# Normed rows and gated products of a two-layer encoder stored in the order in which TensorE loads them

## The chip, the core and the metric

The kernel runs on one core of a Trainium2 chip. The metric is the device time of one execution in microseconds (us); lower is better. The kernel before was run three times, with a median of 1843.3 us (1842.94 to 1844.39).

## What is computed

Two layers of an encoder over 512 frames of 1024 numbers, all in 32-bit floats. Each layer has an attention half (one input projection, retention, differential attention and gated linear attention, one output projection) and a second half, a mixture of 32 SwiGLU experts in 8 groups of 4. Only the second half is touched by the change. Cut to what matters:

```python
h2 = (rms_norm(x, norm2_g[l]) * (1.0 + sc2) + sh2).reshape(B_ * S_, D)
idx, gates = route(h2, router_w, router_b)      # best group, then its best 2 experts
...
def expert_block(args):
    toks, gts, e = args
    xb = h_pad[toks]
    u = jax.nn.silu(xb @ w_gate[e]) * (xb @ w_up[e])
    return (u @ w_down[e]) * gts[:, None]
...
x = x + gt2 * y
```

An expert has weights of 1024x512 (gate), 1024x512 (up) and 512x1024 (down).

## The kernel before, in words

The 512 frames lie in four tiles of 128 frames, frames on the partitions. In each layer the work around the change goes through these stages.

**Residual and routing.** For each tile i the output projection is finished, added to X, squared and summed, and `norm(i)` makes the reciprocal root r2. `route(i)` (from line 1127) then makes the router's scores on VectorE and ScalarE. In it the normed rows X*r2 are written as two parts of the type fp32r, whose products are summed: the high part `xh` (line 1139, ScalarE, one operation of 1024 columns a tile) and the low part `xl`. For tiles 0 and 1 VectorE makes `xl` (line 1141, 1024 columns); for tiles 2 and 3 ScalarE writes X*r2 once more into `xf` (line 1147, two halves of 512) and GpSimd subtracts `xh` (line 1148). From the chosen groups VectorE ranks the groups by size and makes the one-hot matrix `Pt` that puts each frame at a place of its group (line 1298).

**The gather.** `hs`, the normed inputs in the order of the places and turned, is made by matmuls (line 1358): for each of 2 halves of the places (384 columns each), each of 8 blocks k of features, each tile and each of xh and xl one 128x128 stationary operand from the normed rows, with 384 columns of `Pt` streamed past it. That is 128 matmuls in a layer. Eight of them fill one of three PSUM banks, which ScalarE (line 1364, even k) or VectorE (line 1362, odd k) empties. The stationary operand of block k takes every fourth column of a half row:

```python
T.matmul(b, xx[:, i].rearrange("p (q t k) -> p q k t", q=2, k=4)[:, k // 4, k % 4],
         Pt[:, i, c * HP:(c + 1) * HP], ...)
```

so that features which lie next to each other in the weights' rows come from one row of HBM (a partition then holds 4 whole rows of the weight matrix). Then the same `Pt` is streamed past the 4 gate columns of each tile (line 1602).

**The experts.** 32 experts run in a fixed order, alternately one of a large group (places 128 wide, "wide", weights split in two parts by ScalarE and VectorE, three matmuls a block) and one of a small group (64 places, "narrow", the two halves of the columns packed side by side). SyncE issues the weights (line 1435), 1 MB a transfer, into a ring of buffers `R`; `H` are the split parts. For expert e: the gate product, Silu on ScalarE (`es`), the up product, and in `up_part` the gated product `eu` = up * gate weight * Silu in one VectorE operation (line 1489, 512 columns for a wide, 256 for a narrow expert). `turn` transposes `eu` on TensorE halfway through the gate product of the next expert (4 transposes for a wide, 2 for a narrow one), again with a strided stationary operand (every second column), and the down product follows. When a group's four experts are done, `combine` puts its sums back on X: it runs in small steps between the next expert's matmuls, with matmuls against `ePT` and one VectorE addition for each (`u<-u,x`). After the first expert all four engines' instructions are kept in program order, recorded by one helper: they all carry line 122.

Of the kernel before, what the change touches and what calls it, by code (L numbers as in the profile page):

```python
# [15 lines left out]
AF = mybir.ActivationFunctionType  # L16
OP = mybir.AluOpType
# [5 lines left out]
DEPTH, S, D, NT, KD = 2, 512, 1024, 4, 8  # L23
# [116 lines left out]
def hybrid_trunk(ctx: ExitStack, tc: tile.TileContext, x, c, positions, w_mod, b_mod, norm1_g, norm2_g, w_in,  # L140
# [5 lines left out]
    V, A, G, T, SP = nc.vector, nc.scalar, nc.gpsimd, nc.tensor, nc.sync  # L146
# [26 lines left out]
    X = pool(xs, "x0").tile([128, NT, D])  # L173
# [9 lines left out]
    ident = cst("ident")  # L183
# [185 lines left out]
    for l in range(depth):  # L369
        first = l == 0  # L370
        with ExitStack() as ps:
# [104 lines left out]
            for k in range(KD):  # L476
                q, kk = divmod(k, 4)
# [643 lines left out]
            def norm(i):  # L1121
# [2 lines left out]
                V.tensor_scalar(ms, ms, 1.0 / D, EPS, op0=OP.mult, op1=OP.add)  # L1124
                rsqrt(r2s[:, i:i + 1], ms, 1)

            def route(i):

                r2 = r2s[:, i:i + 1]
                lt = rtile([128, NE], "lt")  # L1130
                if i < NT - 1:
                    V.tensor_copy(lt, lp[:, i, 0])
                    yield
                    V.tensor_add(lt, lt, lp[:, i, 1])
                    yield
                V.scalar_tensor_tensor(lt, lt if i < NT - 1 else lp[:, i, 0], r2, lsh, op0=OP.mult, op1=OP.add)
                sc = rtile([128, NE], "sc")
                act(sc, lt, AF.Exp, scale=-1.0)
                A.activation(xh[:, i], X[:, i], AF.Copy, scale=r2)
                if i < NT - 2:  # L1140
                    V.scalar_tensor_tensor(xl[:, i], X[:, i], r2, xh[:, i], op0=OP.mult, op1=OP.subtract)
                else:

                    for n in range(2):
                        cs_ = slice(n * 512, (n + 1) * 512)
                        xf = w2([128, 512], tag="sq", bufs=2)
                        A.activation(xf, X[:, i, cs_], AF.Copy, scale=r2)
                        G.tensor_sub(xl[:, i, cs_], xf, xh[:, i, cs_])
                yield
                V.tensor_scalar(sc, sc, 1.0, None, op0=OP.add)  # L1150
                yield
                V.reciprocal(sc, sc)
                yield
                bi = rtile([128, NG, 4], "bi")
                bif = bi.rearrange("p g e -> p (g e)")
                V.tensor_add(bif, sc, rb)
                yield

                u = rtile([128, NG, 6], "u")
                V.tensor_add(u[:, :, 0:3], bi[:, :, 0:3], bi[:, :, 1:4])  # L1160
                V.tensor_add(u[:, :, 3:5], bi[:, :, 0:2], bi[:, :, 2:4])
                V.tensor_add(u[:, :, 5:6], bi[:, :, 0:1], bi[:, :, 3:4])
                yield
                gs, r1 = rtile([128, NG], "gs"), rtile([128, 1], "r1")
                V.tensor_reduce(gs, u, axis=AX.X, op=OP.max)
                yield
                V.tensor_reduce(r1, gs, axis=AX.X, op=OP.max)
                yield
                V.scalar_tensor_tensor(gs, gs, r1, cst("gidx"), op0=OP.is_equal, op1=OP.mult)
                yield  # L1170
                V.tensor_reduce(r1, gs, axis=AX.X, op=OP.max)
                yield

                pen = rtile([128, NG], "pen")
                V.tensor_scalar(pen, cst("gidx"), r1, NEG, op0=OP.not_equal, op1=OP.mult)
                V.tensor_scalar(grp[:, i], cst("gidx"), r1, None, op0=OP.is_equal)

                T.matmul(pc[:, (i + 1) * NG:(1 + NT) * NG], cst("ones"),
                         grp[:, i, None, :].to_broadcast([128, NT - i, NG]), start=(i == 0), stop=False)
                chosen[i] = sc, bi, pen  # L1180
                yield
# [171 lines left out]
            for c in range(2):  # L1353
                for k in range(KD):
                    b = pbank("x", 3)[:, 0:HP]
                    for i in range(NT):
                        for n, xx in enumerate((xh, xl)):
                            T.matmul(b, xx[:, i].rearrange("p (q t k) -> p q k t", q=2, k=4)[:, k // 4, k % 4],
                                     Pt[:, i, c * HP:(c + 1) * HP], start=(i == 0 and n == 0), stop=(i == NT - 1 and n == 1))
                    dst = hs[:, k, c * HP:(c + 1) * HP]  # L1360
                    if k % 2:
                        V.tensor_scalar(dst, b, hcol[:, 0, k:k + 1], hcol[:, 1, k:k + 1], op0=OP.mult, op1=OP.add)
                    else:
                        A.activation(dst, b, AF.Identity, scale=hcol[:, 0, k:k + 1], bias=hcol[:, 1, k:k + 1])
# [96 lines left out]
            def wide(acc, src, e, amid=None):  # L1461

                r = where[e][0]
                for p in range(4):
                    hl = src.get()
                    for k in range(2):
                        start, stop = p == 0 and k == 0, p == 3 and k == 1
                        if r < NWIDE:
                            three(acc, xTs[r], 2 * p + k, hl, k * 512, start, stop)
                        else:  # L1470
                            halved(acc, hs[:, 2 * p + k, OFFS[r]:OFFS[r] + 64], hl, k * 512, 512, start, stop)
                    step()
                    if amid and p == 1:
                        amid()
# [6 lines left out]
            def up_part(src, e, gacc):  # L1481
                r, j = where[e]
                w = 512 if r < NWIDE else 256
                s = wm.tile([128, FE], tag="es")[:, 0:w]
                A.activation(s, gacc[:, 0:w], AF.Silu)
                acc = pbank("u")
                wide(acc, src, e)
                u_ = wm.tile([128, FE], tag="eu")[:, 0:w]
                V.scalar_tensor_tensor(u_, acc[:, 0:w], gcs[:, r, j:j + 1], s, op0=OP.mult, op1=OP.mult)
                return u_  # L1490

            def turn(u_, e):
                b = pbank("x", 3, [128, 4, 128])
                if where[e][0] < NWIDE:
                    for q in range(4):
                        T.transpose(b[:, q], u_.rearrange("p (q t k) -> p q k t", q=2, k=2)[:, q // 2, q % 2], ident)
                    uT = wm.tile([128, 2, 4, 128], F32R, tag="euT")
                    A.copy(uT[:, 0], b)
                    V.tensor_sub(uT[:, 1], b, uT[:, 0])
                else:  # L1500
                    for k in range(2):
                        T.transpose(b[:, k], u_.rearrange("p (t k) -> p k t", k=2)[:, k], ident)
                    uT = wm.tile([128, 2, 128], tag="euT64")
                    A.copy(uT, b[:, 0:2])
                return uT
# [274 lines left out]
```

## Time and profile before, and how to read them

| | |
|---|---|
| median of 3 runs | 1843.3 us |
| the profiled execution: its own time | 1843.05 us |
| its span, first to last instruction | 1841.2 us |
| busy: PE (matmuls), PEld (weight loads), DVE (VectorE), ACT (ScalarE) | 1765.0, 1270.0, 1095.8, 784.2 us |
| mean granted TensorE clock | 0.981 of 2.4 GHz |
| DMA | 512.12 MB, mean 278 GB/s |

Matmuls overlap in the trace and their ends are modelled, so a busy PE says little; the distance from one start to the next says what a matmul takes in a stream. With a group of n like instructions that lasts s in all, and d for one, that distance is (s - d)/(n - 1). A bracket behind a row is the idle time of the engine before it and what ended it. DVEq, SPq and so on are an engine's sequencer.

### The profile page before, as it was taken

To read this page: it belongs to the slowest core of one execution; us is meant where nothing else is said; L and a number is where in the kernel's file an instruction comes from. 1 tells how busy PE (TensorE), PEld (TensorE's weight loads), DVE (VectorE), ACT (ScalarE), POOL (GpSimd) and SP (SyncE) were. 2 spreads that over 40 slices of the span, in tenths; PEclk is the share of its full clock that TensorE was granted. 3 is DMA by queue.
4 is the path that set the end of the run, shared out by engine and by line. 5 is a ranking of instruction groups with operands and counts; after the bars stand their busy time and mean duration, and the time that the engine had idled before them with its cause. 6 is when DMAs were issued, how large, how long until landed. Compare 5 with 4: busy or idle time off the path is not lost. (4 is left out here: it accounts for less than half of the span.)

```text
span 1841.2 us, 28185 instructions
## 1 busy us (share of the span) xinstructions
PE 1765.0 (96%) x10891; PEld 1270.0 (69%) x10892; DVE 1095.8 (60%) x1968; ACT 784.2 (43%) x1207; POOL 89.4 (5%) x136
## 2 busy tenths in 40 slices
PE   5999999989999999999998999997999999999997
PEld 3866767768665666665748887986966666666673
DVE  3646664464547557566655778656455846756664
ACT  3344442343534443444523555443344444444350
POOL 1010000020000000000000110112000000000000
PEclk9999999998999999999998999998999999999998
DMA  9565547416999999999964211131789999999994
GB/s 333 166 213 191 171 160 226 164 73 253 359 423 378 392 423 367 415 422 353 423 247 141 70 46 47 54 124 51 308 358 422 369 403 422 367 415 419 362 420 179
DMA packets 115617, 512.12 MB, mean 278 GB/s; under 512 B 14978, under 2 KB 42896, under 8 KB 66320
## 3 DMA queue, kind: packets, MB, share of 16 engines
q1 hardware_dynamic: 111952, 504.93, 70.6%
q0 software_dynamic: 1072, 3.32, 0.5%
q10 hardware_dynamic: 2448, 1.94, 0.4%
q8 instruction: 90, 1.47, 0.3%
q14 instruction: 55, 0.45, 0.1%
HBM read 501.73 MB, written 8.42 MB: 277 GB/s over the span
## 5 line engine op out<-in xcount | busy, mean ns | idle before, releaser
L122 DVE TENSOR_TENSOR H<-R,H 128x1024 fp32r<-128x1024 f32 x368 | 431.4, 1221 | 108.9 <-ACT H L122 108.4
L122 ACT CAST H<-R 128x1024 fp32r<-128x1024 f32 x368 | 363.8, 1048 | 47.5 <-DMA R<-in_w_down_dram 28.7
L579 PEld LDWEIGHTS a<-H,u 128*128 128x128 f32 x1728 | 216.5, 190 | 45.0 <-issue 42.2
L579 PE MATMUL a<-H,u 128*128 128x256 f32 x1728 | 245.7, 290 | 0.0
L122 PE MATMUL y<-H,euT 128*128 128x512 f32 x768 | 188.4, 399 | 1.0 <-DVE euT L122 1.0
L122 PE MATMUL g<-H,exT 128*128 128x512 f32 x720 | 183.9, 402 | 0.0
L122 PE MATMUL u<-H,exT 128*128 128x512 f32 x720 | 177.1, 400 | 0.0
L122 PEld LDWEIGHTS y<-H,euT 128*128 128x128 f32 x768 | 141.6, 188 | 46.1 <-ACT H L122 9.2
L122 PEld LDWEIGHTS u<-H,exT 128*128 128x128 f32 x720 | 132.6, 188 | 54.3 <-issue 22.5
L122 PEld LDWEIGHTS g<-H,exT 128*128 128x128 f32 x720 | 131.4, 188 | 36.1 <-issue 8.5
L122 DVE SCALAR_TENSOR_TENSOR eu<-u,u,es 128x256 f32<-128x256 f32 (+1 forms) x62 | 37.9, 612 | 190.3 <-PE u L122 190.3
L122 PE MATMUL g<-R,u 128*64 128x256 f32 x1024 | 126.8, 386 | 0.0
L122 PE MATMUL y<-R,euT 128*64 128x512 f32 x512 | 121.2, 602 | 1.1 <-ACT euT L122 1.1
L122 PE MATMUL u<-R,u 128*64 128x256 f32 x1024 | 118.9, 383 | 0.0
L122 DVE TENSOR_TENSOR u<-u,x 128x512 f32<-128x512 f32 x128 | 84.4, 684 | 45.7 <-PE x L122 45.4
L122 PEld LDWEIGHTS u<-R,u 128*64 128x64 f32 x1024 | 70.1, 137 | 45.3 <-issue 13.9
L122 ACT COPY euT<-x 128x256 f32<-128x256 f32 x32 | 11.9, 373 | 209.9 <-PE x L122 189.3
L122 PEld LDWEIGHTS g<-R,u 128*64 128x64 f32 x1024 | 66.9, 136 | 46.3 <-issue 15.4
L122 PE MATMUL x<-eyh,ePT 128*128 128x512 f32 (+1 forms) x256 | 75.1, 460 | 9.2 <-DVE u L122 5.8
L122 ACT CAST euT<-x 128x512 fp32r<-128x512 f32 x32 | 18.7, 584 | 150.6 <-PE x L122 150.5
L122 PEld LDWEIGHTS y<-R,euT 128*64 128x64 f32 x512 | 32.3, 136 | 63.6 <-issue 52.2
L122 PEld LDWEIGHTS x<-eyh,ePT 128*128 128x128 f32 (+1 forms) x256 | 33.7, 192 | 51.2 <-DVE u L122 31.0
(597 smaller groups left out, 2289.4 us busy)
## 6 DMA issues: line engine op xcount, KB each, us to landing
R<-in_w_gate_dram SPq DMA_DIRECT2D x128, 1024.0 KB
R<-in_w_up_dram SPq DMA_DIRECT2D x128, 1024.0 KB
R<-in_w_down_dram SPq DMA_DIRECT2D x128, 1024.0 KB
M<-in_w_mod_dram SPq DMA_DIRECT2D x80, 512.0 KB
R<-in_w_in_dram SPq DMA_DIRECT2D x20, 1024.0 KB
slab<-in_w_mod_dram SPq DMA_DIRECT2D x16, 512.0 KB
R<-in_w_in_dram SPq DMA_DIRECT2D x24, 256.0 KB
R<-in_w_out_dram SPq DMA_DIRECT2D x4, 1024.0 KB
```

The costliest lines, as they stand in the source:

```text
L122: return self.tc.keep_in_program_order(f(*args, **kw))
L579: T.matmul(acc[i // 2][:, i % 2], a[q][:, k, tk], hl[:, w, k], start=(i % 2 == 0 and q == 0 and k == 0 and n3 == 0), stop=(i % 2 == 1 and ...
```

## The change

The normed rows and the gated products are written to memory in the order in which TensorE will load them. A half row of 512 columns, or a half product of 256, is read in its own order and written permuted: `own` views columns as (t k), `by_rows` as (k t), both walked with t outside and k inside, so that reading is contiguous and each store lands 128 elements after the one before. This is done one half at a time, so each operation of 1024 columns (and `eu` of a wide expert, 512) becomes two. The matmuls of line 1358 and the transposes then take 128 neighbouring columns. What is computed stays the same; GpSimd's subtraction keeps its shape. The path for groups that overflow their places is not touched (it reads its own copies).

```diff
+            def by_rows(a):
+                return a.rearrange("p (k t) -> p t k", k=4)
+            def own(a):
+                return a.rearrange("p (t k) -> p t k", k=4)
...
-                A.activation(xh[:, i], X[:, i], AF.Copy, scale=r2)
+                for n in range(2):
+                    cs_ = slice(n * 512, (n + 1) * 512)
+                    A.activation(by_rows(xh[:, i, cs_]), own(X[:, i, cs_]), AF.Copy, scale=r2)
                 if i < NT - 2:
-                    V.scalar_tensor_tensor(xl[:, i], X[:, i], r2, xh[:, i], op0=OP.mult, op1=OP.subtract)
+                    for n in range(2):
+                        cs_ = slice(n * 512, (n + 1) * 512)
+                        V.scalar_tensor_tensor(by_rows(xl[:, i, cs_]), own(X[:, i, cs_]), r2, by_rows(xh[:, i, cs_]), op0=OP.mult,
+                                               op1=OP.subtract)
                 else:
...
-                        A.activation(xf, X[:, i, cs_], AF.Copy, scale=r2)
+                        A.activation(by_rows(xf), own(X[:, i, cs_]), AF.Copy, scale=r2)
                         G.tensor_sub(xl[:, i, cs_], xf, xh[:, i, cs_])
...
-                            T.matmul(b, xx[:, i].rearrange("p (q t k) -> p q k t", q=2, k=4)[:, k // 4, k % 4],
-                                     Pt[:, i, c * HP:(c + 1) * HP], start=(i == 0 and n == 0), stop=(i == NT - 1 and n == 1))
+                            T.matmul(b, xx[:, i, k * 128:(k + 1) * 128], Pt[:, i, c * HP:(c + 1) * HP],
+                                     start=(i == 0 and n == 0), stop=(i == NT - 1 and n == 1))
...
-                V.scalar_tensor_tensor(u_, acc[:, 0:w], gcs[:, r, j:j + 1], s, op0=OP.mult, op1=OP.mult)
+                for q in range(w // 256):
+                    own = lambda a: a[:, q * 256:(q + 1) * 256].rearrange("p (t k) -> p t k", k=2)
+                    V.scalar_tensor_tensor(u_[:, q * 256:(q + 1) * 256].rearrange("p (k t) -> p t k", k=2), own(acc),
+                                           gcs[:, r, j:j + 1], own(s), op0=OP.mult, op1=OP.mult)
...
-                        T.transpose(b[:, q], u_.rearrange("p (q t k) -> p q k t", q=2, k=2)[:, q // 2, q % 2], ident)
+                        T.transpose(b[:, q], u_[:, q * 128:(q + 1) * 128], ident)
...
-                        T.transpose(b[:, k], u_.rearrange("p (t k) -> p k t", k=2)[:, k], ident)
+                        T.transpose(b[:, k], u_[:, k * 128:(k + 1) * 128], ident)
```

## Rows read from the trace of the kernel before

**Rows 1.** Experts' loop: us, busy PE PEld DVE ACT POOL; PEclk, DMA, GB/s
```profile
500.00:560.00 60.00, 60.00 (x328) 39.69 (x324) 32.88 (x32) 28.65 (x35) 0.00 (x0) 1.00 1.01 422
```

**Rows 2.** Timeline of PE there: start us, us, engine, line, op, operands
```profile
498.41 0.75 PE L122 MATMUL x<-u,eu 128*128 128x128 f32 x4
...
527.61 0.75 PE L122 MATMUL x<-u,eu 128*128 128x128 f32 x4
```

**Rows 3.** Line 1358 alone, both layers: us, PE, PEld, PEclk, DMA, GB/s
```profile
419.00:423.80 4.80, 4.80 (x15) 4.80 (x16) 0.50 0.91 326
424.60:450.00 25.40, 25.40 (x110) 25.32 (x110) 1.00 0.61 256
...
1292.00:1318.30 26.30, 26.30 (x113) 26.15 (x113) 1.00 0.63 263
```

**Rows 4.** Timeline of PEld in the gather
```profile
429.69 18.53 PEld L1358 LDWEIGHTS x<-u,u 128*128 128x128 f32 x79
```

**Rows 5.** Groups of weight loads, whole span: busy us, mean ns, idle before
```profile
L1358 PEld LDWEIGHTS x<-u,u 128*128 128x128 f32 x256 | 62.1, 330 | 6.7 <-issue 3.3 <-DVE u L1298 3.2 <-ACT u L1364 0.2
...
L122 PEld LDWEIGHTS x<-u,eu 128*128 128x128 f32 x192 | 30.0, 205 | 18.6 <-issue 9.2 <-DVE eu L122 3.4 <-DVE u L122 2.2
...
L1602 PEld LDWEIGHTS x<-u,u 128*4 128x4 f32 x32 | 2.7, 86 | 2.7
```

**Rows 6.** Timeline around the gather's end
```profile
450.22 2.72 PEld L1602 LDWEIGHTS x<-u,u 128*4 128x4 f32 x16
...
450.60 3.12 SPq L1435 DMA_DIRECT2D R<-in_w_up_dram  x2
```

**Rows 7.** Timeline of a contiguous load with 256 streamed columns
```profile
199.85 0.90 PEld L579 LDWEIGHTS a<-H,u 128*128 128x128 f32 x7
```

**Rows 8.** The gathers' later parts, all engines, columns as in rows 1
```profile
439.50:450.50 11.00, 11.00 (x49) 10.91 (x49) 1.94 (x3) 2.01 (x3) 0.00 (x0) 1.00 0.04 15
...
1308.50:1318.50 10.00, 10.00 (x44) 10.00 (x44) 1.35 (x2) 2.02 (x3) 0.00 (x0) 1.00 0.01 5
```

**Rows 9.** Waits of SyncE's DMA queue, 440-455 us: us, times, longest
```profile
SPq L1435 <- PE x L1358: 26.8, 1, 26.8
```

**Rows 10.** Timeline, a wide expert's gated product and its transposes
```profile
525.91 0.75 DVE L122 SCALAR_TENSOR_TENSOR eu<-u,u,es 128x512 f32<-128x512 f32 x1 [6.25 <-PE u L122]
...
527.61 0.56 PEld L122 LDWEIGHTS x<-u,eu 128*128 128x128 f32 x4 [0.38 <-issue]
```

**Rows 11.** Timeline of PEld, four transposes of contiguous columns of X
```profile
402.97 0.42 PEld L1102 LDWEIGHTS t<-u,u 128*128 128x128 f32 x4
```

**Rows 12.** Groups of DVE, 480-960 us and 418-470 us: busy us, mean ns
```profile
L122 DVE SCALAR_TENSOR_TENSOR eu<-u,u,es 128x512 f32<-128x512 f32 x15 | 11.2, 750 | 68.6 <-PE u L122 68.6
L122 DVE SCALAR_TENSOR_TENSOR eu<-u,u,es 128x256 f32<-128x256 f32 x16 | 7.7, 483 | 26.3 <-PE u L122 26.3
...
L1302 DVE TENSOR_REDUCE u<-u 128x16 f32<-128x128 f32 x1 | 0.4, 380 | 0.0
...
L1312 DVE TENSOR_REDUCE u<-u 128x8 f32<-128x64 f32 x1 | 0.2, 213 | 0.0
```

**Rows 13.** Timeline of ACT, then of POOL, ahead of the gather
```profile
408.11 1.15 ACT L1139 ACTIVATE u<-u,u 128x1024 fp32r<-128x1024 f32 x1 [0.22 <-DVE u L360]
409.17 0.21 ACT L199 ACTIVATE sc<-lt 128x32 f32<-128x32 f32 x1
409.29 1.32 ACT L1147 ACTIVATE sq<-u,u 128x512 f32<-128x512 f32 x2
...
410.07 2.50 POOL L1148 TENSOR_TENSOR u<-sq,u 128x512 fp32r<-128x512 f32 x2 [2.49 <-ACT sq L1147]
```

**Rows 14.** Timeline, a wide expert's product inside a combine
```profile
592.55 0.74 DVE L122 SCALAR_TENSOR_TENSOR eu<-u,u,es 128x512 f32<-128x512 f32 x1
...
595.07 0.73 PE L122 MATMUL x<-eyh,ePT 64*128 64x512 f32 x3 [0.65 <-DVE u L122]
```

**Rows 15.** Timeline, a narrow expert's product behind a combine
```profile
573.76 0.31 PEld L122 LDWEIGHTS x<-u,eu 128*128 128x128 f32 x2 [0.55 <-DVE eu L122]
```

## The prediction, made before the change was run

> **What bounds the kernel now.** The chain that ended last goes back only through the last few us, so I read by stages, from stretches. In a regular stretch of the experts' loop PE is busy throughout and the DMA engines too [rows 1]. Which of them sets the pace the timeline tells: the four transposes of one wide expert and of the next stand 29.20 us apart [rows 2], the same distance to 0.01 us wherever no group is being put back on X, and PE waits there for almost nothing. TensorE's own sequence is the pace, with the transfers close under it. So a stall of PE in this loop is lost, and work taken off PE there is won as long as weights arrive.
>
> Ahead of the loop each layer has the gather of line 1358: 128 matmuls, PE never idle. It begins at half clock (granted 0.50, 1.2 GHz) with 15 of them in 4.80 us; then at full clock (2.4 GHz) 110 and, in the other layer, 113 were counted [rows 3]. At full clock the distance is (18.53 - 0.33)/78 = 233.3 ns [rows 4, 5]. The reader is to see that this is too long for 384 streamed columns: line 1602 streams the same matrix past stationary operands of 4 columns at (2.72 - 0.086)/15 = 175.6 ns [rows 5, 6]. What differs is the load: 128 columns with a step of 16 bytes last 330 ns each [rows 5], while contiguous 128-column loads come one after the other within 0.90/7 = 129 ns, each beside 256 streamed columns [rows 7]. 233.3/128 is 1.82 ns a column.
>
> **The change part by part.** *Gather.* With contiguous loads the stream becomes the limit. Low end 175.6 ns. High end: 256 columns at 2.4 GHz are 107 ns, so a contiguous pair costs at most 22 ns above its stream [rows 7], and 384 columns (160 ns) cost 182. I take 177, near the row with the same stream: 223 x 56.3 ns = 12.6 us for both layers (11.4 to 12.9). The matmuls at half clock gain nothing: 4.80/15 = 320 ns is 384 columns at 1.2 GHz. I take off 0.5 (0 to 1) for PSUM banks not yet emptied when eight matmuls take 1.42 us instead of 1.87: **-12.1 us**.
>
> Is the earlier end kept? Transfers stop at about 439.5 us with all buffers full, and stand still for 11 us, and 10 us in the second layer [rows 8]; the next issue, at 450.60 us, was released by the gather itself after 26.8 us of waiting [rows 6, 9]. If the gather ends 6 us earlier, SyncE issues 6 us earlier, and the weights for the first expert have still landed 4 us before. PE and transfers move together, so all of it is kept.
>
> *Transposes.* Four loads with a step of 8 bytes take 0.56 us, four contiguous ones 0.42 [rows 10, 11]. The stream between may hide this, so a wide expert's turn gains 0 to 0.14 us, a narrow one's I set at 0. 32 x 0.07 = **-2.2 us** (0 to -4.5).
>
> *Gated products.* From 512 columns in 750 ns and 256 in 483, VectorE's operation costs 216 ns plus 1.04 ns a column [rows 12]. It becomes two for a wide expert, and its stores jump by 512 bytes. No row has such stores. Low end: nothing extra, 1.04 ns (a gain is excluded, since the contiguous store already keeps one column a step). High end: 2.44 ns, GpSimd's 2.50 us for two contiguous operations of 512 [rows 13], the slowest elementwise rate here. Nearest is VectorE reading every fourth column: line 1302 takes 380 ns for 128, where a contiguous 64 take 213 [rows 12] and 128 would take 280: 0.78 ns a column more, 1.82 ns in all, the same as TensorE's strided load. I take 1.82.
>
> A wide product then takes 2 x (216 + 466) = 1.36 us, 0.61 more. Regularly it ends at 526.66 and its transposes start at 527.61 [rows 10]: 0.95 us of matmuls of the next gate product cover it. Without this cover it would cost 0.61 each, 26 times 16 us in all. Two places have none. Three times a layer a wide product stands inside a combine, and behind it in VectorE's queue are a weight split and the addition that PE waits for (0.65 us already) [rows 14]: 6 x 0.61 = 3.7. Three times a layer a narrow product comes late behind the additions and the transposes wait for it [rows 15]: 6 x 0.20 = 1.2. **+4.9 us** (1.3 at the low end, 7.7 at the high).
>
> *Normed rows.* Only tile 3 of each layer is on the path; for tiles 0 to 2 ScalarE's writes, and VectorE's low parts of tiles 0 and 1, stand beside the projection's matmuls, for which both engines wait. Uncovered, each low part would cost 1.0 us (two operations of 216 + 932 ns against 1.28), 3.9 in all. Tile 3's high part takes 1.15 us; two halves like line 1147's take 1.32, and at 0.78 ns a column more 2.1. Behind it stands the exponential that VectorE's ranking needs, and then the products for GpSimd, whose 2.50 us hold VectorE up too [rows 13]. If the exponential comes between the halves, this gains up to 0.4 a layer; if behind both, it costs 1.0, and a later GpSimd up to 0.8 more (at 2.44 ns 2.7 in all). I take 0.8: **+1.6 us** (-0.8 to +5.4). GpSimd's queue and SyncE's get no new instruction.
>
> **Sum.** -12.1 - 2.2 + 4.9 + 1.6 = -7.8 us, against the profiled execution's own 1843.05 us (1.85 above its span; the median of the runs is 1843.3): **1835.3 us**.
>
> **Rivals.** *Stores that cost nothing extra.* [...] Against: both strided rows cost 1.82 ns. Then -12.1 - 2.2 + 1.3 + 0.2 = -12.8: 1830.3 us. Chance 0.20.
>
> *The gain is not kept.* If the loop is paced by transfers and these do not start earlier, the gather's gain waits in front of the first experts' weights, and the late products hide there too; what is left is about 1 us: 1842. For: the DMA share of 1.01 in the loop [rows 1]. Against: the release by the gather [rows 9] and the 10 idle us [rows 8]. Chance 0.05; another 0.03 for all costs at their high ends, which comes to 1842 as well (-12.1 - 2.2 + 7.7 + 5.4 = -1.2).
>
> *Slower: stores slow enough to break the cover.* The place is the 0.95 us between a wide product and its transposes [rows 10]. 750 + 950 = 432 + 512 s gives s = 2.47 ns a stored column; above that each of some 22 regular wide products stalls PE. At 3 ns: 22 x 0.27 = 5.9, inside combines 6 x 1.2 = 7.3, narrow 6 x 0.50 = 3.0, ahead of the gather 2 x 3.3 = 6.6, together 22.8 against 14.3: 1851.6 us. It turns slower at about 2.6. For: no store of this kind is in the trace. Against: no row above 1.82 on VectorE. Chance 0.04. The Trainium skill (Vector Engine (DVE) Microarchitecture Reference, section 5.2) gives 1.71 ns for a destination hopping 4 KiB on every element and 2.50 for steps of 24 words; by 1.71 the forecast would come out about 1 us lower, by 2.50 the cover would just break. No run shown here has such a store.
>
> *The loads do not become shorter.* If what limits the gather were the number of stationary columns and not their step, nothing is won and the costs stay: 1843.05 + 6.5 = 1849.5 us. Against it: 330 ns strided [rows 5] beside loads 129 ns apart [rows 7], both of 128 columns. Chance 0.03. The Trainium skill says just this (TensorE: Matmul & The Clock Gate, section LDWEIGHTS: the time is the columns over 1.2 GHz); by it the strided load would take 107 ns, and this case's trace disagrees.
>
> **How the numbers follow.** The forecast has 0.65. About 0.2% (3.7 us) is what a measurement of this kernel can tell from no change, so faster means below 1839.4. Faster: 0.65 + 0.20 = 0.85. Same: 0.05 + 0.03 = 0.08. Slower: 0.04 + 0.03 = 0.07. Range: down to the free stores with somewhat more from the transposes, 1829.5; up most of the way to all costs at their high ends, 1840.5. It leaves out most of the same and slower cases, 0.15, and about 0.05 below.
>
> **What would show it.** In the profile after: line 1358's loads at about 190 ns instead of 330 and 175 to 182 ns apart at full clock, each gather about 6 us shorter; the idle of the transfers in its later part shrinking from 11 to about 5 us; wide products as two operations of about 0.68 us each (0.48 if stores are free), narrow ones 0.68; regular wide experts still 29.1 to 29.2 us apart; combines about 0.8 us longer. Wrong it would be if the gather's distance stays near 233 ns, if the loop's 29.20 us grow, or if the gather starts over 2 us later than before.

## The result, and the profile after

The changed kernel takes 1834.51 us (median of 6 runs, 1830.62 to 1835.66); the kernel before, on the same chip, 1843.85 us (6 runs, 1842.30 to 1845.29). The ratio is 0.9945, interval 0.9932 to 0.9958. The profiled execution took 1833.86 us, its span is 1832.1 us. Forecast were 1835.3 us.

**The gather.** First the groups of weight loads of the changed kernel, as in [rows 5] (busy us, mean ns of one, idle before); the gather is now line 1370, the gate columns line 1618.

```profile
L1370 PEld LDWEIGHTS x<-u,u 128*128 128x128 f32 x256 | 48.3, 204 | 8.2 <-issue 3.4 <-DVE u L1310 3.3 <-ACT u L1376 1.0
...
L122 PEld LDWEIGHTS x<-u,eu 128*128 128x128 f32 x192 | 21.9, 140 | 21.4 <-issue 9.2 <-DVE eu L122 4.8 <-DVE u L122 2.2
...
L1618 PEld LDWEIGHTS x<-u,u 128*4 128x4 f32 x32 | 2.7, 85 | 2.7
```

A load of the gather fell from 330 to 204 ns, one of the transposes from 205 to 140; the 4-column loads, which the change leaves alone, stay at 85. The timeline of PE in the gather of the changed kernel (start, us, operation, count):

```profile
427.77 18.32 PE L1370 MATMUL x<-u,u 128*128 128x384 f32 x104
445.93 1.38 PE L1618 MATMUL x<-u,u 128*4 128x384 f32 x7
```

(445.93 - 427.77)/104 = 174.6 ns from one start to the next, as line 1602 had with 4 columns [rows 6]: now the stream limits. From its first to its last matmul the gather takes 24.85 us in either layer, where it took 31.19 and 30.86. Together that is 12.35 us less.

**Do the transfers follow?** A stretch in the gather's last part (us, busy time of PE, PEld, DVE, ACT, POOL; PEclk, DMA, GB/s), and SyncE's queue (timeline, then waits):

```profile
442.00:446.00 4.00, 4.00 (x25) 3.91 (x24) 0.68 (x1) 1.31 (x2) 0.00 (x0) 1.00 0.00 0
```

```profile
446.13 3.10 SPq L1447 DMA_DIRECT2D R<-in_w_up_dram  x2
```

```profile
SPq L1447 <- PE x L1370: 20.7, 1, 20.7
```

The queue is still released by the gather, after 20.7 us instead of 26.8 [rows 9], and the transfers stand still for about 4.4 us (from 441.7 us to the issue at 446.13) instead of 11 [rows 8]. The first group of the gate product follows the last gather matmul at 3.8 us, where it followed at 3.9. So the gather's gain is kept.

**Ahead of the gather.** ACT and POOL of the changed kernel, to be read beside [rows 13]:

```profile
410.22 1.17 ACT L1148 ACTIVATE u<-u,u 128x512 fp32r<-128x512 f32 x1 [0.22 <-DVE u L360]
411.19 0.22 ACT L199 ACTIVATE sc<-lt 128x32 f32<-128x32 f32 x1
411.28 1.16 ACT L1148 ACTIVATE u<-u,u 128x512 fp32r<-128x512 f32 x1
412.25 2.07 ACT L1159 ACTIVATE sq<-u,u 128x512 f32<-128x512 f32 x2
...
413.45 2.49 POOL L1160 TENSOR_TENSOR u<-sq,u 128x512 fp32r<-128x512 f32 x2 [3.77 <-ACT sq L1159]
```

The exponential came between the halves, 0.97 us behind the start of the high part (1.06 before). GpSimd's products begin 3.23 us behind it, 1.27 us later than before. Small VectorE operations that fall into those 2.49 us take 1.0 to 1.2 us instead of 0.2, in both kernels, and now others of the ranking fall in, for instance (timeline of DVE in the changed kernel):

```profile
413.50 1.24 DVE L1181 SCALAR_TENSOR_TENSOR gs<-gs,r,u 128x8 f32<-128x8 f32 x1
```

The gather begins 18.26 us after the last matmul of the output projection, not 17.98, and 18.17, not 17.90, in the second layer: +0.55 us in all.

**Products and turns.** VectorE's product in a regular stretch, and PE's transposes there (timelines), then the group of all products (busy us, mean ns):

```profile
521.24 1.17 DVE L122 SCALAR_TENSOR_TENSOR eu<-u,u,es 128x256 f32<-128x256 f32 x2 [6.26 <-PE u L122]
```

```profile
493.84 0.66 PE L122 MATMUL x<-u,eu 128*128 128x128 f32 x4
...
522.94 0.66 PE L122 MATMUL x<-u,eu 128*128 128x128 f32 x4
```

```profile
L122 DVE SCALAR_TENSOR_TENSOR eu<-u,u,es 128x256 f32<-128x256 f32 x92 | 56.9, 672 | 191.5 <-PE u L122 191.5
```

An operation of 256 columns takes 672 ns instead of 483, but two of them behind each other 1.17 us, not 1.34: they overlap by 0.17 us. Wide experts turn 29.10 us apart (29.20 before): the transposes' 0.66 us instead of 0.75 are won. Their four loads take 0.42 us (timeline of PEld), where they took 0.56 [rows 10]:

```profile
522.94 0.42 PEld L122 LDWEIGHTS x<-u,eu 128*128 128x128 f32 x4 [0.38 <-issue]
```

Around a combine it goes the other way. First the turns of the kernel before, then of the changed one (timeline of PE): the last before a narrow expert's late product, that expert, and the wide expert behind it.

```profile
556.82 0.75 PE L122 MATMUL x<-u,eu 128*128 128x128 f32 x4
573.77 0.50 PE L122 MATMUL x<-u,eu 128*128 128x128 f32 x2
595.73 0.74 PE L122 MATMUL x<-u,eu 128*128 128x128 f32 x4
```

```profile
552.05 0.66 PE L122 MATMUL x<-u,eu 128*128 128x128 f32 x4
569.19 0.44 PE L122 MATMUL x<-u,eu 128*128 128x128 f32 x2 [0.29 <-DVE eu L122]
591.42 0.66 PE L122 MATMUL x<-u,eu 128*128 128x128 f32 x4
```

16.95 and 21.96 us became 17.14 and 22.23: +0.19 and +0.27. Why, VectorE and PE of the changed kernel show inside the combine:

```profile
587.90 1.16 DVE L122 SCALAR_TENSOR_TENSOR eu<-u,u,es 128x256 f32<-128x256 f32 x2
588.89 1.22 DVE L122 TENSOR_TENSOR H<-R,H 128x1024 fp32r<-128x1024 f32 x1
590.03 1.27 DVE L122 TENSOR_TENSOR u<-u,x 128x512 f32<-128x512 f32 x2
```

```profile
590.76 0.73 PE L122 MATMUL x<-eyh,ePT 64*128 64x512 f32 x3 [0.97 <-DVE u L122]
```

The product is 0.42 us longer, the weight split and the addition behind it come later, and PE waits 0.97 us for them instead of 0.65 [rows 14]. Six combines times 0.46 us are 2.8 us; that is what the shorter transposes win, and from the first to the last turn the loop takes 0.08 us more in the first layer and 0.56 in the second (0.41 of it at one place, told of under *mixed*).

### The profile page after: what moved, and what is told of

Its sections match the earlier page's. It is cut to its first block, busy times and chain, and to the rows that moved or that the text cites. A ratio compares the mean times of both kernels' runs of the same rounds, so it can differ in the third digit from the quotient of the medians.

```text
span 1832.1 us, 28257 instructions
## 1 busy us (share of the span) xinstructions
PE 1751.1 (96%) x10891; PEld 1252.5 (68%) x10892; DVE 1113.6 (61%) x2004; ACT 795.5 (43%) x1215; POOL 88.9 (5%) x136
## 3 DMA queue, kind: packets, MB, share of 16 engines
q8 instruction: 89, 1.46, 0.3%
## 5 line engine op out<-in xcount | busy, mean ns | idle before, releaser
L122 DVE SCALAR_TENSOR_TENSOR eu<-u,u,es 128x256 f32<-128x256 f32 x92 | 56.9, 672 | 191.5 <-PE u L122 191.5
```

The costliest lines, as they stand in the source:

```text
L122: return self.tc.keep_in_program_order(f(*args, **kw))
```

## The experiments

From each profile, by the starts of PE's matmuls: the start of the last output-projection matmul of layer 0; from there to the gather (both layers); the gather from first to last matmul; and by how much the loop from the first to the last turn is longer than before.

| kernel | projection ends, us | ahead of gather, us | gather, us | loop against before, us | median, us | ratio to before |
|---|---|---|---|---|---|---|
| before | 401.01 | 17.98, 17.90 | 31.19, 30.86 | | 1843.9 to 1844.5 | |
| after | 402.65 | 18.26, 18.17 | 24.85, 24.85 | +0.08, +0.56 | 1834.51 | 0.9945 |
| rows_only | 402.69 | 18.26, 18.19 | 24.74, 24.83 | -0.12, +0.06 | 1832.48 | 0.9931 |
| products_only | 402.67 | 17.97, 17.90 | 31.20, 30.91 | +0.12, +0.18 | 1845.41 | 1.0005 |
| mixed | 402.86 | 18.26, 18.17 | 24.96, 24.82 | -0.57, -0.25 | 1832.78 | 0.9931 |
| strided_reads | 401.26 | 18.25, 18.17 | 24.91, 24.86 | -1.05, -0.49 | 1830.21 | 0.9923 |
| one_product | 402.09 | 18.27, 18.19 | 25.00, 24.83 | -0.74, -1.17 | 1830.74 | 0.9928 |
| all_reads | 401.50 | 19.44, 19.35 | 24.98, 24.84 | -0.78, -1.31 | 1832.19 | 0.9937 |
| after_again | 404.14 | 18.26, 18.19 | 24.85, 24.85 | +0.05, +0.18 | 1834.59 | 0.9945 |
| one_product_again | 402.70 | 18.27, 18.18 | 24.91, 24.86 | -1.44, -1.38 | 1830.50 | 0.9924 |

An interval reaches about 0.0014 to either side of a ratio of this table, 2.5 us, but 0.0009 for products_only. The stages of the table from the projection's end on repeat to 0.1 or 0.2 us, but for single places in the loops, told of under *mixed*; the projection's end does not.

**Half the change each.** *rows_only* keeps the permuted rows and the contiguous gather and takes products and transposes back:

```diff
-                for q in range(w // 256):
-                    own = lambda a: ...
-                    V.scalar_tensor_tensor(u_[:, q * 256:(q + 1) * 256].rearrange("p (k t) -> p t k", k=2), own(acc),
-                                           gcs[:, r, j:j + 1], own(s), op0=OP.mult, op1=OP.mult)
+                V.scalar_tensor_tensor(u_, acc[:, 0:w], gcs[:, r, j:j + 1], s, op0=OP.mult, op1=OP.mult)
...
-                        T.transpose(b[:, q], u_[:, q * 128:(q + 1) * 128], ident)
+                        T.transpose(b[:, q], u_.rearrange("p (q t k) -> p q k t", q=2, k=2)[:, q // 2, q % 2], ident)
```

> Normed rows permuted and gather contiguous, gated products and their transposes as before. Theory (the gather carries the gain, the products cancel out): gather 24.85 us a layer instead of 31.0, so -12.3, and +0.55 for the later gather starts: 11.5 to 12 us faster than before (ratio about 0.9937), regular wide turns 29.20 us apart. Rival (the products carry part of the gain): 9 us or less faster, and slower than the whole change by 2 us or more. Rival (the 1.7 us that the changed kernel lost in the first 82 us of its profile belong to the normed rows): that start is late by 1.7 us here too, else within 0.5 us of before.

*products_only* is the reverse.

> Gated products written permuted in operations of 256 and transposes of contiguous columns; normed rows and gather as before. Theory: turns -0.09 us x 26 to 32 = -2.3 to -2.9, narrow late products and wide products inside combines +0.46 x 6 = +2.8: within 1 us of before (ratio 0.9995 to 1.0005). Rival (products help): 2.5 us faster, combines as long as before. Rival (products hurt as the prediction's sum had it, 4.9 - 2.2): 2.7 us slower.

rows_only is 11.7 us faster than before (1844.19 to 1832.48), its turns are 29.20 us apart, as its timeline of PE shows:

```profile
493.85 0.75 PE L122 MATMUL x<-u,eu 128*128 128x128 f32 x4
...
523.05 0.75 PE L122 MATMUL x<-u,eu 128*128 128x128 f32 x4
```

products_only is as long as before: ratio 1.0005 (0.9996 to 1.0014), its loops 0.12 and 0.18 us longer. The 2.7 us that the prediction's terms for turns and products add up to are excluded by the loops of its profile, and so are the 2.5 us of a gain. The gather carries the gain, the products cancel out. The start of the span is late by 1.7 us in both, in the half without permuted rows too, so the third theory, that the rows cost it, falls.

**What the combines lost.** *mixed* writes the twelve uncovered products in one contiguous operation and turns them with a step:

```diff
+            def plain(e):
+                r, j = where[e]
+                return (r, j) in [(g, 0) for g in range(1, NWIDE)] + [(NWIDE + g, 3) for g in range(NWIDE - 1)]
...
+                if plain(e):
+                    V.scalar_tensor_tensor(u_, acc[:, 0:w], gcs[:, r, j:j + 1], s, op0=OP.mult, op1=OP.mult)
+                    return u_
```

> The whole change, but the twelve products that nothing covers (six narrow ones that come late, six wide ones inside combines) are written in one contiguous operation as before and transposed with a step. Theory (these stores are what the combines lost): 2.3 to 2.8 us faster than the whole change (ratio to before about 0.9932), the turns around a combine as far apart as before. Rival (the combines lost by their shifted phase against the transfers, not by the stores): as long as the whole change, and the turns keep their +0.46 us.

The same three turns in its timeline:

```profile
552.39 0.66 PE L122 MATMUL x<-u,eu 128*128 128x128 f32 x4
569.34 0.50 PE L122 MATMUL x<-u,eu 128*128 128x128 f32 x2
591.30 0.74 PE L122 MATMUL x<-u,eu 128*128 128x128 f32 x4
```

16.95 and 21.96 us apart, as in the kernel before: it was the product's new form, its stores and its cut in two together. Its loops are 0.65 and 0.81 us shorter than after's, 1.5 in all, not 2.3 to 2.8. The difference is two late narrow products, one in each layer, that came 0.44 and 0.64 us later again; after has one such place in its second layer, 0.41 us later than its others. At each of them the timeline of ACT shows the cast of a weight block waiting for its transfer, once in after, then twice in mixed:

```profile
1546.91 2.00 ACT L122 CAST H<-R 128x1024 fp32r<-128x1024 f32 x2 [1.73 <-DMA R<-in_w_gate_dram]
```

```profile
810.66 2.00 ACT L122 CAST H<-R 128x1024 fp32r<-128x1024 f32 x2 [1.76 <-DMA R<-in_w_gate_dram]
...
1673.26 2.00 ACT L122 CAST H<-R 128x1024 fp32r<-128x1024 f32 x2 [1.95 <-DMA R<-in_w_gate_dram]
```

At the other five such places after waits 1.03 us at most, at the other four mixed waits 0.88, and nothing comes late. strided_reads and one_product have one of 0.4 us or more each, behind waits of 1.76 and 1.98 us. So weights that come late ahead of a combine cost 0.4 to 0.7 us each, in some profiles and not in others; what makes a transfer late there was not traced. Without the three places mixed's loops would be 2.1 us shorter than after's, near what was expected. By the times of the runs, mixed (1832.78) can't be told from after (1834.51): the intervals overlap.

**Jumping reads in place of jumping stores.** *strided_reads* turns the product's access around; the operands are read in the order (k, t), and the store is contiguous:

```diff
-                    own = lambda a: a[:, q * 256:(q + 1) * 256].rearrange("p (t k) -> p t k", k=2)
-                    V.scalar_tensor_tensor(u_[:, q * 256:(q + 1) * 256].rearrange("p (k t) -> p t k", k=2), own(acc),
+                    own = lambda a: a[:, q * 256:(q + 1) * 256].rearrange("p (t k) -> p k t", k=2)
+                    V.scalar_tensor_tensor(u_[:, q * 256:(q + 1) * 256].rearrange("p (k t) -> p k t", k=2), own(acc),
```

> The whole change, but the gated product reads PSUM and the gate with a step of 8 bytes and stores contiguous columns, instead of the other way round. Theory (a column costs by the jump, on whichever side, 1.8 ns): products of 256 columns last 0.65 to 0.69 us as in the whole change, and the time is the same to 0.5 us. Rival (only a jumping store costs): products last 0.48 us, a wide one ends 0.85 to 1.0 us after its start, and the kernel is 2 us faster than the whole change. Rival (reads pay twice, for two operands): 0.9 us or more each, the cover of 0.5 us is broken and the kernel is 5 us or more slower than the whole change.

The group of products and a regular wide product of its trace:

```profile
L122 DVE SCALAR_TENSOR_TENSOR eu<-u,u,es 128x256 f32<-128x256 f32 x92 | 41.8, 480 | 189.7 <-PE u L122 189.7
```

```profile
519.90 0.88 DVE L122 SCALAR_TENSOR_TENSOR eu<-u,u,es 128x256 f32<-128x256 f32 x2 [6.26 <-PE u L122]
```

480 ns, as contiguous (483 [rows 12]): the theory and the rival of costly reads fall, the rival in which only the jumping store costs holds here (the loops are 2.18 us shorter than after's). Reading PSUM and SBUF with a step of 8 bytes costs VectorE nothing, storing with jumps of 512 bytes had cost (672 - 480)/256 = 0.75 ns a column. Two operations now take 0.88 us where one of 512 took 0.75 [rows 10]. So of the 0.42 us that the change added to a wide product 0.13 is the split and 0.29 the stores. No run stores with a step of 8 bytes, so this one doesn't tell whether it is the side that matters or the length of the step; *all_reads* below points to the step.

With the reads permuted the split isn't needed: in the order (k, m), with m over both halves of the tokens, the operand has two dimensions. *one_product*:

```diff
+                V.scalar_tensor_tensor(u_.rearrange("p (k m) -> p k m", k=2), acc[:, 0:w].rearrange("p (m k) -> p k m", k=2),
+                                       gcs[:, r, j:j + 1], s.rearrange("p (m k) -> p k m", k=2), op0=OP.mult, op1=OP.mult)
...
+                        T.transpose(b[:, q], u_[:, (q % 2) * 256 + (q // 2) * 128:][:, 0:128], ident)
```

> The whole change, but the gated product is one operation again, of 512 columns for a wide expert, reads with a step of 8 bytes and stores contiguous columns; the transposes read contiguous columns. Theory (a strided read is free, a strided store and the split cost): wide products 0.75 us and narrow 0.48 as before the change, regular pairs of turns 29.10 us apart, combines as long as before the change: 0.5 to 1 us faster than with strided reads in two operations, some 14 us faster than before (ratio about 0.992). Rival (over 256 strided steps the read does cost): wide products 0.95 us or more, no gain over the two operations.

Groups of its trace:

```profile
L122 DVE SCALAR_TENSOR_TENSOR eu<-u,u,es 128x512 f32<-128x512 f32 x30 | 22.6, 752 | 137.6 <-PE u L122 137.6
L122 DVE SCALAR_TENSOR_TENSOR eu<-u,u,es 128x256 f32<-128x256 f32 x32 | 15.4, 483 | 51.1 <-PE u L122 51.1
```

Products take 752 and 483 ns, as before the change, and the ratio is 0.9928 (0.9914 to 0.9941). That is within the interval of strided_reads, so the expected 0.5 to 1 us between those two was not seen in the runs. Its loops are 1.91 us shorter than before's, with one place of 0.66 us more like those in mixed; strided_reads' are 1.54 shorter, with one of 0.44. Without these two places it would be 2.57 and 1.98, 0.6 us apart, as expected.

To compare it with the change itself, both ran again on one chip.

> The whole change once more, beside one_product_again on the same chip. Theory: 9.5 to 11 us faster than before; the 1.7 us by which its first profile was later than before's by 82 us come from how the first transfers fall and vary from run to run, so here anything from 0 to 2 us of them; combines +0.46 us longer each, as in the first profile. Rival (the change itself costs them): 1.5 to 1.9 us again.

> One operation, strided reads, contiguous stores, beside the whole change on the same chip. Theory: 2.8 us faster than the whole change (the six combines no longer 0.46 us longer; ratio to before lower by 0.0015). Rival (within the scatter of the first transfers nothing is left): within 1 us of it.

after_again: 1834.59 us (1833.06 to 1835.44); one_product_again: 1830.50 (1829.76 to 1831.56). All five runs of the one lie below all five of the other: 4.1 us, of which the loops of the profiles explain 3.05 (-1.44 - 1.38 against +0.05 + 0.18). The two profiles' own spans are 3.99 us apart (1832.74 and 1828.75): the start, which lies ahead of every product, gives 1.43 of it, and behind the loops 0.4 is given back. So about 3 of the 4.1 us are shown to be the product's. The timeline of PE of one_product_again at the combine:

```profile
552.17 0.66 PE L122 MATMUL x<-u,eu 128*128 128x128 f32 x4
569.15 0.44 PE L122 MATMUL x<-u,eu 128*128 128x128 f32 x2
591.05 0.66 PE L122 MATMUL x<-u,eu 128*128 128x128 f32 x4
```

16.98 and 21.90 us: the combine's loss is gone, and the transposes' gain stays. This version beats both kernels. From its last turn of layer 0 to the last output projection of layer 1 it takes 0.7 us more than before; in the other profiles this stretch is between 0.5 us shorter and 0.6 longer, so whether a part of the gain is given back there is not shown.

after_again also shows the start to be scatter. First a line of the waits of PE in the first 90 us of after, then the same of after_again (us in total, times, longest us):

```profile
PE m L322 <- DMA slab<-in_w_mod_dram: 7.6, 4, 6.4
```

```profile
PE m L322 <- DMA slab<-in_w_mod_dram: 8.8, 4, 7.2
```

In the kernel before they are 7.3 us, the longest 5.5. These are the first transfers, ahead of everything that the change touches; in the table the projection of layer 0 ends 0.25 to 3.13 us later than in the profile of before in all nine others, which is therefore itself an early one; the changed kernel alone has 1.64 and 3.13.

**Normed rows by reads.** *all_reads* adds the same to the rows, where the step is 16 bytes: the high part in one operation of 1024, the low parts of tiles 0 and 1 in one, the halves for GpSimd.

```diff
+                xi, xo = X[:, i].rearrange("p (m k) -> p k m", k=4), [z[:, i].rearrange("p (k m) -> p k m", k=4) for z in (xh, xl)]
+                A.activation(xo[0], xi, AF.Copy, scale=r2)
...
+                    V.scalar_tensor_tensor(xo[1], xi, r2, xo[0], op0=OP.mult, op1=OP.subtract)
```

> As one_product, and the normed rows too are written by operations that read with a step (16 bytes) and store contiguous columns, high part in one operation of 1024. Theory (reads are free on ScalarE and VectorE): high part 1.15 us instead of two of 1.2, low part 1.28 instead of two of 1.15, the two halves for GpSimd 0.71 instead of 1.15: the gather starts 17.9 us after the last output projection as before the change, 0.5 us gained in all against one_product. Rival (a 16-byte read step costs, as the reduction over every fourth column in the kernel before, 380 ns for 128): high part 1.9 to 2.2 us, no gain or up to 1 us a layer lost.

The rival held. Groups of its trace (busy us, mean ns):

```profile
L1140 ACT ACTIVATE u<-u,u 128x1024 fp32r<-128x1024 f32 x8 | 17.0, 2130 | 1.8 <-DVE u L360 1.5
...
L1148 ACT ACTIVATE sq<-u,u 128x512 f32<-128x512 f32 x8 | 9.4, 1196 | 0.0
...
L1142 DVE SCALAR_TENSOR_TENSOR u<-u,u,u 128x1024 fp32r<-128x1024 f32 x4 | 8.2, 2059 | 5.4 <-ACT u L1140 5.4
```

Contiguous, in the kernel before:

```profile
L1139 ACT ACTIVATE u<-u,u 128x1024 fp32r<-128x1024 f32 x8 | 9.2, 1150 | 0.8 <-DVE u L360 0.6
L1147 ACT ACTIVATE sq<-u,u 128x512 f32<-128x512 f32 x8 | 5.5, 708 | 0.0
...
L1141 DVE SCALAR_TENSOR_TENSOR u<-u,u,u 128x1024 fp32r<-128x1024 f32 x4 | 5.1, 1285 | 2.4 <-ACT u L1139 2.4
```

So reads of 16 bytes cost ScalarE (2130 - 1150)/1024 = 0.96 ns a column and VectorE 0.76, about as much as the jumping stores: 0.75 on VectorE, and on ScalarE (1151 - 708)/512 = 0.87, by this group of the changed kernel:

```profile
L1159 ACT ACTIVATE sq<-u,u 128x512 f32<-128x512 f32 x8 | 8.6, 1151 | 0.0
```

The exponential now stands behind one operation of 2.1 us, and the gather begins 1.46 and 1.45 us later than before the change, 1.2 us a layer later than in one_product, a little over the bound that was set. This is the loss that the prediction feared from the permuted rows; what spares the change is that its high part is cut in two and the exponential goes between.

**What a load costs by its step.** Both take the kernel before and change the gather's operand alone, for example

```diff
-                            T.matmul(b, xx[:, i].rearrange("p (q t k) -> p q k t", q=2, k=4)[:, k // 4, k % 4],
+                            T.matmul(b, xx[:, i].rearrange("p (t k) -> p k t", k=8)[:, k],
```

> The kernel before, with the gather's stationary operand read with a step of 8 bytes instead of 16; it pairs other columns of the rows with the weights, so the output is another. Theory (a load's time grows with its step; at 8 bytes the transposes had 140 ns a load, under the 160 ns of the stream): the stream limits, 173 to 176 ns apart, each gather 24.9 us. Rival (any step that is not 1 costs the whole 1.82 ns a column): 233 ns, 31 us.

> The kernel before, with the gather's stationary operand read with a step of 32 bytes instead of 16; other columns, another output. Theory (the load fetches pieces of a fixed size, and at 16 bytes each column already costs one): 233 ns apart, loads about 330 ns, as with 16 bytes. Rival (the load pays for the distance): 400 ns apart or more, each gather 50 us.

The timeline of PEld with a step of 8 bytes (gather_step2), then with 32 (gather_step8):

```profile
427.86 17.10 PEld L1358 LDWEIGHTS x<-u,u 128*128 128x128 f32 x98
444.94 2.68 PEld L1602 LDWEIGHTS x<-u,u 128*4 128x4 f32 x16
```

```profile
427.81 23.49 PEld L1358 LDWEIGHTS x<-u,u 128*128 128x128 f32 x97
451.20 0.80 PEld L1602 LDWEIGHTS x<-u,u 128*4 128x4 f32 x5
```

17.08/98 = 174.3 ns with 8 bytes, loads 211 ns on average: the stream limits, as with contiguous columns. 23.39/97 = 241 ns with 32 bytes, loads 338 ns: nearly what 16 bytes cost (233 and 330). The first gather takes 24.78 and 32.02 us, where it took 31.19. Both theories held. What 8 bytes cost the gather hides, as the stream is the longer; the transposes show it: four loads in 0.56 us with 8 bytes, 0.42 contiguous. So the price rises up to a step of 16 bytes and hardly beyond. Pieces of about that size would fit these four steps; a price by distance doesn't. Both took much longer as a whole (1991.31 and 2006.86 us), since the second layer then routes other tokens and runs the matmuls for tokens beyond the places, which the kernel before skips; only the first gather is compared.

*gather_step1* has contiguous loads and natural rows:

```diff
+                            T.matmul(b, xx[:, i, k * 128:(k + 1) * 128],
```

> The kernel before with contiguous gather loads and nothing else: the rows stay in their own order, so other columns are paired with the weights and the output is another. Theory (the permuted rows cost 0.27 us a layer ahead of the gather, and nothing of the gather's gain depends on them): first gather 24.85 us long, beginning 17.98 us after the last output projection as in the kernel before, not 18.26. Rival (the later start has another cause, such as the shifted phase): 18.2 to 18.3 here too.

The timeline of PEld in its first gather:

```profile
427.92 17.10 PEld L1358 LDWEIGHTS x<-u,u 128*128 128x128 f32 x98
445.01 2.68 PEld L1602 LDWEIGHTS x<-u,u 128*4 128x4 f32 x16
```

(445.01 - 427.92)/98 = 174.4 ns. The gather takes 24.92 and 24.83 us in the two layers and begins 17.98 and 17.91 us after the projection, to 0.01 us as before the change. So the permuted rows are what put it off by 0.28, and the time that the gather gains comes from the load's step alone. As a whole it took 1832.15 us (one run).

## Why the prediction was right, point by point

- **Gather, -12.1 us: right.** 12.35. Taken were 177 ns a matmul, measured 174.6; the discount of 0.5 us for PSUM banks was a little large. The high end of 182 ns stood on 0.90/7 = 129 ns for contiguous loads [rows 7]; each of them lasts 0.19 us in the trace, so their starts are (0.90 - 0.19)/6 = 118 ns apart. The 177 did not rest on it. gather_step1 shows that the load's step alone does it. The rival in which only the number of columns counts is refuted: with 128 columns each, the matmuls of the gather stood 174, 174, 233 and 241 ns apart at steps of 4, 8, 16 and 32 bytes. That rival is the rule of the Trainium skill (TensorE: Matmul & The Clock Gate, section LDWEIGHTS); these runs disagree with it.
- **Kept: right.** SyncE's queue was released after 6.1 us less of waiting (20.7 for 26.8), the still time of the transfers shrank to 4.4 us. The rival of transfers that pace the loop is out for this size of gain; only the late weight blocks, at 0.4 to 0.7 us each, show how close they are.
- **Transposes, -2.2 us: right, a little small.** A pair of turns fell by 0.10 us, of which the wide expert has nearly all; over the 26 to 32 wide turns 2.5 to 3. one_product_again, where the products last as long as before, has loops 2.82 us shorter.
- **Gated products, +4.9 us: mechanism right, size too large; 2.8.** A jumping column costs 1.04 + 0.75 = 1.79 ns, taken were 1.82. (The Trainium skill, Vector Engine (DVE) Microarchitecture Reference, section 5.2, gives 1.71 for a destination hopping 4 KiB and 2.50 for steps of 24 words. The 1.79 of the jumps of 512 bytes here is near the former.) The narrow term was hit (0.19 for 0.20). The wide one failed in "2 x (216 + 466) = 1.36 us, 0.61 more": the two operations overlap by 0.17 us, so that it was 0.42 more, and PE's wait grew by 0.32, of which the shorter transposes gave back a part: 0.27 for 0.61. The row that I called nearest, VectorE reading every fourth column, had the right price, though for a store, and for reads of 16 bytes like its own, but not for the reads of 8 bytes, which are free. The cover of 0.95 us held: the regular wide turns came closer together.
- **Normed rows, +1.6 us: too large; 0.55.** The exponential came between the halves, the better of the two cases named, and gained 0.09 us, not up to 0.4; GpSimd came 1.27 us later, to which the rest of the later start, about 0.3 a layer, is put down by the rows alone. That GpSimd's products hold VectorE up was right, though [rows 13] don't show VectorE. For tiles 0 to 2 no cost is seen: the projection of layer 0 ends at 402.69 us with permuted rows (rows_only) and at 402.67 without (products_only). The term of 0.8 a layer lay between the cases; the better one held.
- **The sum.** By stages (the gather, its later start, the way from it to the first turn, the loops) after's profile gives -12.35 + 0.55 - 0.1 + 0.64 = -11.3 us (after_again -11.7), where -7.8 was forecast: the terms that were mis-sized erred to one side, by 3.5 us. The spans of the two profiles are only 9.1 us apart (1841.2 and 1832.1), because after's start was 1.64 us later and the stretches behind its two loops were 0.5 us longer together, terms that the forecast did not have. The measured differences of medians are 9.3 and 9.9 us. So the forecast of 1835.3 came within 0.8 us partly by luck: of the 3.5 us that the terms gave too little 2 did not reach the medians, and another 0.8 lay in the profile of before, on which the sum stood: it had an early start and was 0.8 to 1.4 us below the medians of its later runs. What share the start has in the medians, where no stages are on record, stays open.
- **The rivals.** "Stores that cost nothing extra" gave 1830.3 us. Stores do cost. But strided_reads, one_product and one_product_again do without jumping stores in the products (the rows keep them) and take 1830.21, 1830.74 and 1830.50.

## What to carry to other kernels

When a layout has to be changed between two engines, put the jump where it is free: here VectorE's reads with a step of 8 bytes cost nothing, while its jumping stores, reads of 16 bytes on VectorE and ScalarE, and TensorE's loads of 16 bytes (330 against 204 ns) all cost 0.75 ns a column and more. A store with a step of 8 bytes was not tried. Compare the distance of matmuls with what their stream needs; where it is longer, look at the load's operand, and first at whether its step is 16 bytes or more. A longer operation off PE costs little where a regular stretch covers it, and nearly its whole price in the few places, here the combines, where its engine's queue is what PE waits for: price it place by place, and give only those places the other form, unless there is a form, like the reads of 8 bytes here, that costs nothing anywhere.

## What the runs showed of the hardware that was not expected

- The step matters up to 16 bytes: in the gather, whose stream hides what a load takes under about 174 ns, loads of 128 columns lasted 204, 211, 330 and 338 ns at 4, 8, 16 and 32 bytes; four transposes' loads took 0.42 us contiguous and 0.56 at 8. VectorE's reads were free at 8 bytes (480 ns for 256 columns against 483 contiguous) and cost 0.76 ns a column at 16.
- Two independent VectorE operations of 256 columns in a row take 0.88 us, not 2 x 0.48: the second starts 0.40 us after the first.
- ScalarE pays for jumps on either side: 512 columns took 708 ns contiguous, 1151 with jumping stores, 1196 with reads of 16 bytes.
